# One encoder layer on one core: a new table for the order and the buffers of a kernel that replays its operations

## The chip, the cores and the metric

The kernel runs on one core of one Trainium2 chip. A core has TensorE (PE; its weight loads are listed as PEld), VectorE (DVE), ScalarE (ACT), GpSimd (POOL) and SyncE (SP), each with its own instruction queue, and 16 DMA engines, which SyncE, ScalarE and GpSimd issue transfers to. The metric is the device time of one execution in microseconds (us), as a median of several runs.

## The reference

One layer of a bidirectional encoder trunk in float32, for 512 rows of width 1024 (x is 1 x 512 x 1024):

```python
h = rmsnorm(x, mix_norm)
rx, ry, qkv, z, ba, gates = jnp.split(h @ w_in, SPLIT_IDX, axis=-1)
y_rnn = rglru_branch(rx, ry, ...) @ w_rnn_proj
y_dn = deltanet_branch(qkv, z, ba, ...) @ w_dn_proj
g_rnn, g_dn = jnp.split(jax.nn.sigmoid(gates), 2, axis=-1)
x = x + (g_rnn * y_rnn + g_dn * y_dn) @ w_out
h = rmsnorm(x, ffn_norm)
gt, up = jnp.split(h @ w_gate_up, 2, axis=-1)
x = x + (jax.nn.silu(gt) * up) @ w_down
return rmsnorm(x, final_norm)
```

The first branch is a short convolution, two sigmoid gates from block-diagonal matmuls and a linear scan in both directions. The second is a gated delta rule over 8 heads in chunks of 64 rows, in both directions; for each chunk it solves a unit triangular system of 64 x 64:

```python
A = jnp.where(strict, jnp.einsum("nhcid,nhcjd->nhcij", kb, k) * decay, 0.0)
lhs = A + jnp.eye(CHUNK)
u = triangular_solve(lhs, v * beta, lower=True, unit_diagonal=True)
w = triangular_solve(lhs, kb * exp(gc), lower=True, unit_diagonal=True)
```

## The kernel before

**What it computes on.** All matmuls with large operands work on pairs of a high and a low part (a value rounded to TensorE's faster float32 form, and the rest), so that three products stand for one in float32; several matrices are multiplied with seven block products in place of eight. Most matmuls are 128 x 128 weights on 128 x 512 or 128 x 256 columns. Buffers in SBUF are of two sizes, t2 (2 KB in each partition) and t4 (4 KB); a tile in PSUM is called ps and is one of eight banks. `hh` and `hl` hold the high and low part of the normalised, transposed input.

**The head.** SyncE and ScalarE load x in halves (`xl_`). While the first loads are on the way, TensorE does 16 matmuls of a matrix of ones on itself into a tile `idle`, whose result nobody reads. `load_gain` brings the norm's weights in as eight rows and transposes them (`gain1r`, `gain`). `raw_transpose` (L634) transposes x before it is normalised, four times 128 x 128 into one ps tile, and ScalarE copies the result, scaled by `gain`, into the high part `rhi` (float32 in the fast form), VectorE the rest into `rlo`; the first products (with the blocks of `w_in`) start from these. `rms_rstd` (L602) takes the squares (one half of the row on ScalarE, one on VectorE) and the root. The cast of a weight block into its high part is ScalarE's, too.

**The inverses.** `dn_inverse(g)` (L1052) inverts the triangular blocks of a group g of two heads; there are four groups. VectorE inverts the 32 x 32 diagonal blocks, TensorE puts them together: first 32 matmuls of 32 x 32 into a bank `pr`, a scaled copy of it by ScalarE, then 48 of 32 x 32 into two banks `px` and `pz`:

```python
for p8 in range(8):
    for b0 in (0, 2):
        for d, (i0, i1) in enumerate(((b0, b1), (b1, b0))):
            rr = R[32 * i1:32 * i1 + 32, 32 * p8:32 * p8 + 32]
            T.matmul(px[...], rr, yd(d, i1, p8), ..., tile_position=(32 * i1, 32 * i0))
            if b0 == 2 * d:
                T.matmul(pz[...], yd(d, i1, p8), rr, ..., tile_position=(32 * i1, 32 * i1))
```

then, after copies by ScalarE, 16 matmuls of 64 x 64 into `pr2` and 16 into `px2`. Each of these matmuls is in plain float32 and shows as two records in the trace; they take some hundredths of a microsecond each, where a matmul of 128 x 512 takes over two tenths. The same time of the program holds other work that TensorE does between them: products of `w_in` with `hh` and `hl`, transposes (`turn`, weights `ident`), products of the gates.

**Low parts by transfers.** The low parts of sums of weight blocks are made in place by transfers that GpSimd issues and that add to what the tile holds (rows `t<-t` POOLq in the profile).

**What sets the order.** No call to an engine runs at once. `Rec` records every call as an operation, in the order of the program's text, and `Plan.emit` (L482) issues them in the order of a table, `ORDER`, of 9257 numbers (each operation once). All engines' operations stand in this one list, so the list gives every engine's queue its order. A second table, `HOMES`, has for every t2, t4 and ps tile, in the order in which `new` (L546) draws them, the number of the buffer that it is put in; `emit` adds a wait where a tile takes a buffer whose last user was another engine. Both tables were found by a search outside the kernel. All instructions carry L516, the line of the recorder that runs the call.

Of the kernel before, what the change touches and what calls it, by code (L numbers as in the profile page):

```python
# [31 lines left out]
2061 0 2 3 5 2062 140 10 11 14 2063 2079 12 13 2080 1 2065 65 2099 2117 2100 7 234 2118 97 96 143 2064 2066 70 158 152  # L32
151 17 18 19 20 21 22 23 24 25 26 27 28 29 30 31 32 33 41 34 35 15 36 42 43 44 16 37 39 2067 2068 2073 2074 2075 2076
2069 2070 38 57 58 49 50 51 52 59 60 2077 2071 66 2081 45 2083 40 2072 2085 2078 2091 67 47 2082 2084 68 2092 2086
2087 2101 2102 71 72 69 73 75 74 312 53 77 2093 76 78 48 46 54 2103 61 55 62 56 2119 79 2094 2095 2088 2096 2111 2089
88 80 81 2098 2121 2090 2104 63 82 2097 9 85 89 84 92 64 93 83 2120 2122 90 86 2112 2113 2105 2106 2107 2108 2109 2110
2114 2115 2116 2123 2124 2129 2130 2131 2132 2125 2133 2134 390 363 2126 2127 159 160 235 2128 161 162 163 164 237 364
91 1123 1092 2138 418 3804 609 915 2142 94 313 87 2135 99 100 95 104 105 165 238 239 240 241 166 242 167 168 243 244
245 169 170 171 315 316 317 246 318 319 247 248 249 236 172 173 174 175 250 251 252 320 321 322 323 253 324 325 326
327 254 255 256 257 258 98 101 102 106 103 107 155 259 124 108 109 110 111 132 116 391 1124 314 125 328 133 117 134  # L40
126 135 127 118 119 392 2139 329 176 112 330 144 114 6 147 331 332 333 177 113 1093 142 141 146 157 145 122 123 115
260 334 335 336 337 261 365 136 120 121 128 130 138 156 131 137 129 139 3806 1126 262 1127 1128 178 179 338 339 180
181 340 1095 341 417 342 343 344 345 1096 263 264 265 266 267 268 1097 1098 3805 1099 269 270 271 272 273 274 182 183
346 347 184 348 148 349 350 275 149 276 277 278 351 352 185 186 187 188 1100 189 279 280 190 191 285 474 759 762 2136
760 150 1125 3807 203 286 192 1101 353 354 582 528 355 356 357 358 359 360 361 362 393 394 395 763 396 397 398 193
1102 1103 1104 1105 399 400 401 402 403 404 861 916 2140 367 2137 1247 2141 1031 1185 1000 368 1094 369 370 3808 768
583 216 281 282 283 194 195 196 197 284 289 205 610 371 1129 1130 1131 1132 198 199 200 204 206 287 207 584 405 290
201 475 1133 1134 1135 1136 1137 1138 1139 1140 1141 381 1142 1143 406 407 408 409 410 411 412 413 414 415 1144 372
888 862 291 366 288 208 292 864 416 865 529 421 3809 422 423 1106 373 385 386 387 382 1145 1146 1147 383 866 293 384
867 1107 1108 1109 1110 531 532 868 210 424 211 294 209 212 773 533 534 535 536 1111 388 295 374 869 307 308 309 213  # L50
214 215 218 870 375 376 537 807 3810 296 217 863 783 219 476 297 298 310 1112 299 300 301 1186 1113 1114 1115 419 425
636 377 378 889 667 420 379 530 764 1116 1117 871 872 873 1118 1119 1120 303 1148 1149 304 585 874 875 876 305 586 587
302 444 380 611 1150 877 769 306 445 588 589 538 765 439 590 591 592 426 431 432 433 593 594 595 612 440 389 434 448
435 436 774 770 539 766 767 771 772 441 437 1121 540 541 761 784 427 428 878 879 880 881 1151 1152 778 882 429 776 438
442 555 556 883 884 885 886 542 543 637 449 779 153 453 596 544 477 478 887 479 480 481 482 483 484 485 775 786 443
890 892 430 452 447 451 787 893 597 598 311 1187 894 154 895 780 1122 1216 545 599 600 601 788 1188 602 603 604 605
606 607 608 613 546 547 548 486 487 549 488 1189 1190 550 1191 551 1153 552 553 614 891 454 1192 1193 1194 1195 668
450 1196 554 1197 489 446 792 669 777 781 782 790 557 1001 797 490 1198 1199 1200 1201 1202 1203 1204 1205 670 671 672
673 674 675 676 677 678 679 680 681 682 683 684 685 686 1206 491 1207 1208 1209 492 493 789 791 615 502 3811 501 793
455 559 896 897 902 898 899 903 560 1248 468 798 1002 561 904 5595 562 616 558 799 563 564 8 617 905 494 495 496 497  # L60
498 499 500 505 910 911 912 1210 1211 913 577 578 1212 469 579 580 565 566 567 568 573 574 575 576 1249 506 1154 639
640 569 570 571 900 687 688 623 507 618 901 624 689 619 690 733 202 1066 906 572 691 692 693 907 625 626 620 908 909
621 785 794 802 581 470 917 472 803 1589 943 795 622 641 642 627 643 503 644 628 629 1250 1251 918 919 920 921 922 923
1252 456 508 462 942 944 509 924 694 914 631 632 1253 1254 1255 925 926 927 928 929 930 931 1256 1257 633 932 933 934
1258 1259 1260 1261 1262 1263 1264 1265 1266 1267 1268 511 935 936 937 1269 1270 1271 1272 734 808 810 811 812 645 646
647 796 698 800 801 805 804 806 1535 1534 457 458 504 463 464 471 466 473 510 1213 465 630 634 699 1032 938 939 940
834 835 700 1273 523 515 648 649 516 524 813 814 525 650 512 513 1214 517 1217 1274 1275 514 941 809 815 816 817 459
818 819 519 520 521 651 652 526 518 946 522 1588 1034 1003 820 821 822 823 824 825 826 827 828 829 830 701 1004 1005
831 1006 1035 653 654 1036 1037 1038 1039 1040 1041 945 638 1215 467 460 738 740 747 736 729 730 1007 655 656 657 658
659 660 661 1008 1009 1010 1011 1219 1012 732 735 737 3013 3014 739 1013 1014 1015 1016 1017 832 702 833 1220 1221  # L70
1222 703 838 1223 1224 1018 1019 1020 1021 1022 1023 1024 1025 1033 1225 1226 1042 1227 1043 969 1228 527 947 635 948
949 1218 748 461 836 1276 839 1026 970 731 749 950 840 841 951 1044 1045 1561 1643 1507 1046 1047 1048 1049 1050 1051
1052 750 1027 1508 842 1229 1230 1231 972 973 974 975 662 952 953 1232 1053 1054 1055 1056 1057 1233 1234 960 837 954
961 843 1277 971 1463 1397 704 705 751 964 706 707 965 708 709 966 752 1615 976 977 978 979 741 753 754 1235 742 755
757 756 663 955 1155 967 1562 1067 1236 1237 1238 1239 844 962 845 846 963 847 956 957 980 981 982 983 984 985 958 959
1058 710 711 1028 1156 1157 1240 1241 1242 1243 1158 1159 1160 1161 848 849 850 1162 856 857 852 858 859 853 854 1616
855 851 1063 986 987 988 989 990 991 992 993 994 995 1564 1565 1566 1510 1163 1164 1165 1166 1167 1567 1642 743 745
695 1509 1168 1169 1170 1171 1172 1173 1174 1175 1176 1177 1178 1179 1180 744 1062 746 1353 1354 1568 3015 1074 860
3016 664 1617 1563 665 1244 758 1059 1355 666 1590 1181 1511 1644 1029 1080 4 1070 1064 696 1065 1068 1512 1513 1514
1515 1516 1618 1619 1517 1245 968 1441 2148 1331 1620 1518 1519 1281 1520 1521 1569 1246 1522 1570 1571 1572 1573 1574  # L80
3017 3018 1575 3019 1576 712 713 714 715 716 717 718 719 720 721 722 1621 1622 1623 1624 1625 1626 1627 1628 1629 723
724 227 228 1577 1578 1332 2144 229 1579 1580 1030 1182 1398 725 1356 697 1523 1524 1581 1582 1357 1583 1584 1585 1586
1587 1075 1076 1078 1358 1525 1526 1527 1528 1529 1530 1531 1532 1533 3020 3021 3022 3023 3024 1334 1359 1630 1631
1183 996 997 726 230 2355 1669 2348 1069 1592 727 1184 1077 1593 728 1399 1594 1632 1633 1634 1635 1360 1536 1071 1464
1060 1072 1645 1595 998 3199 3025 1335 1636 1637 231 232 220 221 222 223 224 1638 1639 1640 1641 1336 1337 1338 1400
1401 1402 3026 3027 1403 1339 1361 1591 1081 1079 999 3198 1538 1646 1086 1061 3028 3029 1465 1333 3030 3031 3032 3033
3034 3035 3036 1647 1648 1362 1404 1405 1278 1280 1596 1539 1540 1279 1406 1407 1363 1364 1365 1597 1366 1367 1368
1340 1341 1342 1343 1344 1345 1346 1347 1348 1408 1409 1410 1411 1412 1369 1370 1349 1350 1351 1413 3037 3038 3039
# [1836 lines left out]
```

## Time and profile before

| what | us |
|---|---|
| median of 3 runs | 1040.49 |
| lowest and highest run | 1038.98, 1211.41 |
| the profiled execution | 1040.44 |
| its span, first to last instruction | 1038.7 |
| granted TensorE clock, mean | 0.997 |
| ScalarE busy | 730.5 (70%) |
| VectorE busy | 906.1 (87%) |

The profiled execution agrees with the median, so its rows can be used for the sum as they are. A row of the page names engine, tile written and read, shape, count, busy time and idle time ahead; a row of the chain has its start, its length and what it was; a row of the timeline gives start, length, engine, operation and count, and in brackets the idle time ahead of it and what ended it ("issue" when the trace shows nothing that it waited for). A row of a table by windows gives the stretch and its length, busy time and instruction count of the engines in it, the clock granted (1.00 is full), the DMA engines' share and GB/s.

### The profile page before, as it was taken

The page shows a single profiled execution, that of the slowest core. Times are in us where ns is not written, and L with a number is a line of the kernel's source. Part 1 is how long each engine was busy: PE and PEld are TensorE (multiplying, and loading weights), DVE is VectorE, ACT ScalarE, POOL GpSimd, SP SyncE. Part 2 cuts the span into 40 slices and gives each one's busy share as a digit, 9 for nine tenths or more (in the row PEclk, how much of TensorE's full clock was granted, in tenths as well). Part 3 has the DMA queues.
Part 4 walks back from the last instruction along what each step waited for, and adds up shares of the span by engine and source line. Part 5 has one row for each costly group of instructions (what it writes and reads, how often), then busy time and mean ns, then how long its engine had stood idle before and what let it go on. Part 6 is the DMA issues. An engine that isn't in the chain of part 4 may idle for free.

```text
span 1038.7 us, 18051 instructions
## 1 busy us (share of the span) xinstructions
PE 1028.2 (99%) x6675; PEld 902.0 (87%) x6675; DVE 906.1 (87%) x1699; ACT 730.5 (70%) x1331; POOL 91.1 (9%) x145
## 2 busy tenths in 40 slices
PE   9999999999999999999999999999999999999997
PEld 8988888888888888798888888889999999998886
DVE  6899998959896589659859979999999998999998
ACT  8699999998457766798897565578444544455674
POOL 6000000112000111142212000000000000000000
PEclk9999999999999999999999999999999999999999
DMA  9952442325644125979985636976555332256532
GB/s 300 308 159 85 144 120 85 90 56 127 183 96 122 50 80 151 267 177 219 232 222 134 183 114 213 304 217 200 166 174 173 118 102 82 83 203 198 180 109 81
DMA packets 185512, 163.75 MB, mean 158 GB/s; under 512 B 7728, under 2 KB 156352, under 8 KB 185424
## 3 DMA queue, kind: packets, MB, share of 16 engines
q1 hardware_dynamic: 178752, 144.37, 46.0%
q0 software_dynamic: 5344, 14.82, 7.9%
q10 hardware_dynamic: 1328, 3.42, 0.9%
q8 instruction: 52, 0.85, 0.3%
q14 instruction: 36, 0.29, 0.1%
HBM read 133.18 MB, written 18.91 MB: 146 GB/s over the span
## 4 chain that ended last, share of the span: by engine, by line
PE 98%; ACT 1%; DMA 0%; issue 0%; DVE 0%; ACTq 0%; DVEq 0%
PE ps L516 98%; ACT t L516 1%; DMA t<-in_w_in_dram 0%; ACTq L516 0%; DVE t L516 0%; ACT L516 0%; DVE na L516 0%; DVEq L1920 0%; DVE so L516 0%; ACT so L516 0%; ACT rst L516 0%; ACT warm L516 0%; DVE rin L516 0%
## 5 line engine op out<-in xcount | busy, mean ns | idle before, releaser
L516 PE MATMUL ps<-t,t 128*128 128x512 f32 (+3 forms) x3039 | 536.0, 322 | 2.5 <-issue 1.6
L516 DVE TENSOR_TENSOR t<-t,t 128x512 fp32r<-128x512 f32 (+19 forms) x807 | 506.3, 658 | 27.8 <-ACT t L516 13.4
L516 PEld LDWEIGHTS ps<-t,t 128*128 128x128 f32 (+1 forms) x3039 | 430.6, 180 | 58.2 <-issue 2.7
L516 PE MATMUL ps<-hh,t 128*128 128x512 f32 (+2 forms) x1680 | 456.5, 347 | 0.0
L516 ACT CAST t<-t 128x512 fp32r<-128x512 f32 (+2 forms) x400 | 298.0, 780 | 158.9 <-DVE t L516 60.5
L516 PEld LDWEIGHTS ps<-hh,t 128*128 128x128 f32 (+1 forms) x1680 | 298.1, 189 | 38.2 <-ACT t L516 0.2
L516 PE MATMUL ps<-hl,t 128*128 128x512 f32 (+2 forms) x848 | 278.6, 347 | 0.0
L516 PEld LDWEIGHTS ps<-hl,t 128*128 128x128 f32 (+1 forms) x848 | 158.4, 189 | 19.5 <-issue 0.2
L516 ACT ACT_TABLE_LOAD x73 | 93.7, 1283 | 12.0 <-DVE so L516 5.1
L516 DVE SCALAR_TENSOR_TENSOR t<-ps,par,t 128x511 f32<-128x511 f32 (+1 forms) x108 | 79.3, 744 | 14.7 <-ACT t L516 13.7
L516 ACT COPY t<-ps 128x512 f32<-128x512 f32 (+3 forms) x108 | 44.3, 429 | 52.7 <-PE ps L516 51.4
L516 ACT ACTIVATE t<-t 128x128 f32<-128x128 f32 (+5 forms) x114 | 72.6, 647 | 9.8 <-DVE t L516 8.0
L516 DVE TENSOR_TENSOR t<-ps,t 128x256 f32<-128x256 f32 (+1 forms) x106 | 50.3, 486 | 11.4 <-PE ps L516 8.7
L516 DVE TENSOR_TENSOR t<-t 128x512 f32<-128x512 f32 (+1 forms) x81 | 51.0, 636 | 0.9 <-DMA t<-in_w_out_dram 0.6
L516 ACT ACTIVATE t<-ps,par 128x512 f32<-128x512 f32 x68 | 45.8, 707 | 7.4 <-PE ps L516 7.2
L516 POOL TENSOR_SCALAR_AFFINE_SELECT t<-t 128x512 f32<-128x512 f32 x32 | 25.6, 807 | 218.5 <-DMA t<-gcr 107.5
L516 PE MATMUL ps<-t,na 128*128 128x128 f32 (+2 forms) x640 | 42.9, 232 | 0.0
L516 PEld LDWEIGHTS ps<-t,na 128*128 128x128 f32 (+2 forms) x640 | 39.6, 145 | 3.8 <-issue 1.4
L516 ACT ACTIVATE t<-ps 128x512 f32<-128x512 f32 (+1 forms) x58 | 28.7, 508 | 15.5 <-PE ps L516 15.0
L516 PE MATMUL ps<-ident,t 128*128 128x128 f32 (+1 forms) x200 | 32.4, 276 | 0.3 <-DVE t L516 0.3
L516 POOL DMA_DIRECT2D t<-t x20 | 18.1, 938 | 146.4 <-ACT t L516 131.3
L516 DVE SCALAR_TENSOR_TENSOR t<-ps,negc,t 128x128 f32<-128x128 f32 x48 | 13.7, 344 | 19.0 <-PE ps L516 18.9
(151 smaller groups left out, 612.4 us busy)
## 6 DMA issues: line engine op xcount, KB each, us to landing
t<-in_w_in_dram SPq DMA_DIRECT2D x70, 512.0 KB, 5.2
t<-in_w_gate_up_dram SPq DMA_DIRECT2D x44, 512.0 KB, 5.0
t<-in_w_down_dram SPq DMA_DIRECT2D x22, 512.0 KB, 4.9
t<-t POOLq DMA_DIRECT2D x20, 512.0 KB, 6.0
t<-in_w_down_dram SPq DMA_DIRECT2D x33, 256.0 KB, 3.8
t<-in_w_out_dram SPq DMA_DIRECT2D x12, 512.0 KB, 6.0
t<-in_w_rnn_proj_dram SPq DMA_DIRECT2D x16, 384.0 KB, 3.6
sums<-t SPq DMA_DIRECT2D x11, 512.0 KB, 4.1
```

Source lines behind the costliest of these rows:

```text
L516: self.plan.ops.append((self.eng, {x.tensor.name for x in aps}, outs, lambda: real(*a, **kw)))
```

## The change

The two tables have other numbers. The rest of the program is the same, text and operations. Of ORDER's and HOMES' rows, the first ones show how it looks:

```diff
 ORDER = """
-2061 0 2 3 5 2062 140 10 11 14 2063 2079 12 13 2080 1 2065 65 2099 2117 2100 7 234 2118 97 96 143 2064 2066 70 158 152
+2 0 17 18 19 20 21 22 23 5 3 2061 2062 10 11 14 1 2079 2080 13 12 2099 7 153 2100 2118 2117 234 96 2063 2064 70 2065
...
 HOMES = """
-1 3 2 4 3 0 10 17 11 18 1 2 7 6 5 7 6 8 9 0 10 12 13 11 14 7 6 8 0 2 1 30 2 0 7 6 0 0 9 23 1 12 6 2 14 1 14 1 4 7 6 1
+0 3 1 2 1 0 9 15 10 18 2 3 6 7 5 7 4 6 8 1 9 11 12 13 14 5 22 30 26 15 31 27 4 7 6 0 1 0 8 23 2 11 2 14 1 11 5 6 14 2
...
```

What it does is seen in the queues. The instructions of each engine are the same ones, but for four loads of ScalarE's tables fewer (69 for 73), which the order of functions decides.

**The head.** TensorE's queue before begins so (`ps_95` is the tile `idle`; `ps_102` and `ps_103` take the transposes of x, `t_88` and `t_90`; `ps_597` and `ps_598` are the first products, of weights `t_600` and `t_601` with the high part `t_98`):

```order
L516 MATMUL ps_95<-ones_83 128x128 x16
L516 MATMUL ps_102<-ident_78,t_88 128x128
L516 MATMUL ps_103<-ident_78,t_88 128x128
L516 MATMUL ps_102<-ident_78,t_90 128x128
L516 MATMUL ps_102<-ident_78,t_88 128x128
L516 MATMUL ps_93<-ident_78,gain1r_92 128x8
L516 MATMUL ps_102<-ident_78,t_90 128x128
L516 MATMUL ps_103<-ident_78,t_90 128x128
L516 MATMUL ps_103<-ident_78,t_88 128x128
L516 MATMUL ps_103<-ident_78,t_90 128x128
L516 MATMUL ps_597<-t_600,t_98 128x512
```

and after so:

```order
L516 MATMUL ps_95<-ones_83 128x128 x11
L516 MATMUL ps_93<-ident_78,gain1r_92 128x8
L516 MATMUL ps_95<-ones_83 128x128 x2
L516 MATMUL ps_102<-ident_78,t_88 128x128
L516 MATMUL ps_102<-ident_78,t_90 128x128
L516 MATMUL ps_102<-ident_78,t_88 128x128
L516 MATMUL ps_102<-ident_78,t_90 128x128
L516 MATMUL ps_95<-ones_83 128x128 x2
L516 MATMUL ps_103<-ident_78,t_88 128x128
L516 MATMUL ps_95<-ones_83 128x128
L516 MATMUL ps_103<-ident_78,t_90 128x128
L516 MATMUL ps_103<-ident_78,t_88 128x128
```

Five of the sixteen matmuls on ones now stand among the transposes, the gain's transpose comes first, and `ps_102` is complete before `ps_103` begins; one more transpose, and then the first products, follow. ScalarE's queue at the same place, before:

```order
L516 ACT_TABLE_LOAD
L516 CAST t_600<-t_599 128x512
L516 ACT_TABLE_LOAD
L516 ACTIVATE warm_87<-eps_t_86 128x1
L516 CAST t_600<-t_599 128x512
L516 ACTIVATE t_110,ssq_106<-t_88 128x512
L516 ACTIVATE t_116,ssq_112<-t_90 128x512
L516 ACTIVATE t_98<-ps_102,gain_94 128x256 x2
```

and after (the first cast is of half a weight block, the `ssq` rows are the squares, the last row the scaled copies):

```order
L516 ACT_TABLE_LOAD
L516 ACTIVATE warm_87<-eps_t_86 128x1
L516 CAST t_600<-t_599 128x512
L516 ACTIVATE t_116,ssq_112<-t_90 128x512
L516 CAST t_600<-t_599 128x512
L516 ACTIVATE t_110,ssq_106<-t_88 128x512
L516 ACTIVATE t_98<-ps_102,gain_94 128x256 x2
```

One table load is gone there (the next now comes some thirty rows later), and the two casts stand ahead of one square each. On SyncE's queue the second half of the second weight block (`t_602`) moves ahead of the second halves of x, which stood ahead of it.

**Group 1 of the inverses.** TensorE's queue before, with what each instruction waits for, at the start of the matmuls into `pr` (here `ps_805`; `t_802` and `t_803` are VectorE's inverses, `t_1003` is a low part added by a transfer of GpSimd):

```order
L516 MATMUL ps_1004<-hh_96,t_1003 128x512 [waits DMASW4_49]
L516 MATMUL ps_1004<-hh_96,t_1003 128x512
L516 MATMUL ps_1106<-hh_96,t_1104 128x512
L516 MATMUL ps_1004<-hh_96,t_1003 128x512 x4
L516 MATMUL ps_1106<-hl_97,t_1104 128x512
L516 MATMUL ps_1004<-hh_96,t_1003 128x512
L516 MATMUL ps_1106<-hh_96,t_1104 128x512
L516 MATMUL ps_1004<-hh_96,t_1003 128x512
L516 MATMUL ps_616<-t_619,t_621 128x512 [waits DMAHW6_49,PE_49]
L516 MATMUL ps_805<-t_802,na_789 32x32 [waits DVE_49,Activation_49]
L516 MATMUL ps_805<-t_803,na_789 32x32
```

and after:

```order
L516 MATMUL ps_1004<-hh_96,t_1002 128x512
L516 MATMUL ps_1004<-hl_97,t_1002 128x512
L516 MATMUL ps_1004<-hh_96,t_1003 128x512 [waits DMASW6_49]
L516 MATMUL ps_1004<-hh_96,t_1003 128x512 x7
L516 MATMUL ps_805<-t_802,na_789 32x32 [waits DVE_49]
L516 MATMUL ps_805<-t_803,na_789 32x32
```

The product with the DMA's block `t_619` has gone elsewhere, and of the waits ahead of the run two are left. Further on, the 48 matmuls into `px` and `pz` (`ps_808`, `ps_807`) ended before with

```order
L516 MATMUL ps_808<-t_806,t_803 32x32
L516 MATMUL ps_808<-t_806,t_802 32x32
L516 MATMUL ps_883<-ident_78,t_867 128x128
L516 MATMUL ps_1106<-hl_97,t_1104 128x512
L516 MATMUL ps_1106<-hh_96,t_1104 128x512
L516 MATMUL ps_616<-t_620,t_621 128x512
L516 MATMUL ps_617<-t_619,t_621 128x512
L516 MATMUL ps_616<-t_619,t_622 128x512 x2
L516 MATMUL ps_617<-t_620,t_621 128x512
L516 MATMUL ps_617<-t_619,t_621 128x512
L516 MATMUL ps_809<-t_804,na_789 64x64 x16
```

and are now split, 31 of them ahead of this piece and 17 behind its long matmuls:

```order
L516 MATMUL ps_808<-t_806,t_803 32x32
L516 MATMUL ps_808<-t_806,t_802 32x32
L516 MATMUL ps_883<-ident_78,t_867 128x128
L516 MATMUL ps_1106<-hl_97,t_1104 128x512
L516 MATMUL ps_616<-t_620,t_621 128x512
L516 MATMUL ps_1106<-hh_96,t_1104 128x512
L516 MATMUL ps_1106<-hl_97,t_1104 128x512
L516 MATMUL ps_616<-t_619,t_621 128x512
L516 MATMUL ps_616<-t_620,t_621 128x512
L516 MATMUL ps_1106<-hh_96,t_1104 128x512
L516 MATMUL ps_616<-t_619,t_622 128x512 x2
L516 MATMUL ps_617<-t_619,t_621 128x512
```

**Group 0.** Before, the run into `pr` (`ps_692`) was followed by a transpose and then by 50 long matmuls before the run into `px` (`ps_695`) and `pz`, of which these are the first:

```order
L516 MATMUL ps_692<-t_689,na_676 32x32
L516 MATMUL ps_692<-t_690,na_676 32x32
L516 MATMUL ps_770<-ident_78,t_754 128x128
L516 MATMUL ps_589<-t_560,t_591 128x512
L516 MATMUL ps_589<-t_524,t_592 128x512
L516 MATMUL ps_589<-t_530,t_592 128x512
```

Now eight are left between the two runs:

```order
L516 MATMUL ps_692<-t_690,na_676 32x32
L516 MATMUL ps_771<-ident_78,t_754 128x128
L516 MATMUL ps_569<-t_548,t_572 128x512
L516 MATMUL ps_569<-t_554,t_572 128x512
L516 MATMUL ps_866<-hl_97,t_864 128x512
L516 MATMUL ps_866<-hh_96,t_864 128x512
L516 MATMUL ps_866<-hl_97,t_864 128x512
L516 MATMUL ps_569<-t_560,t_572 128x512
L516 MATMUL ps_866<-hh_96,t_864 128x512
L516 MATMUL ps_866<-hl_97,t_864 128x512
L516 MATMUL ps_695<-t_693,t_690 32x32
L516 MATMUL ps_695<-t_693,t_689 32x32
```

In groups 0, 1 and 3 single transposes now also stand inside the short runs; in group 2 the 64 x 64 matmuls into `pr2` follow the run into `px` and `pz` at once, where before twelve long matmuls stood between, and six long ones are left between `pr2` and `px2`, where eight were.

858 rows, old and new, of tables (HOMES, ORDER) are left out of this document.

## The prediction, made before the run

> **What bounds the kernel now.** I read the page first, for shares, then the chain that ended last, then the waits of TensorE, and last the timeline and the windows around each place where the chain leaves TensorE. The page:
>
> ```profile
> span 1038.7 us, 18051 instructions
> PE 1028.2 (99%) x6675; PEld 902.0 (87%) x6675; DVE 906.1 (87%) x1699; ACT 730.5 (70%) x1331; POOL 91.1 (9%) x145
> ```
>
> TensorE is busy 99% of the span. The chain, in order of time (start, length, what):
>
> ```profile
> 0.80 3.91 DMA t<-in_w_in_dram
> 4.74 0.62 ACT t L516
> 5.37 1.28 ACT L516
> ...
> 9.03 417.90 PE ps L516 x2289
> 426.93 1.60 issue
> 428.53 197.78 PE ps L516 x1534
> ...
> 633.00 398.49 PE ps L516 x2665
> ```
>
> So the whole execution is one queue of matmuls, with three places to win: the 9.03 us ahead of the first long matmul, a hole of 1.60 us at 426.93, and 1038.7 - 1031.5 = 7.2 us of tail. The other engines only matter where they hold TensorE up, and that is little: the first row below is the hole, the second lies ahead of 9.03.
>
> ```profile
> PE ps L516 <- issue: 1.6, 1, 1.6
> PE ps L516 <- ACT t L516: 0.9, 1, 0.9
> ```
>
> **The change part by part.** Only the order of the 9257 operations and their buffers change; TensorE has the same matmuls. How long they take does not depend on the order where they stand back to back:
>
> ```profile
> 50.00:100.00 50.00, 50.00 (x222) 1.00 0.44 139
> ```
>
> 222 long matmuls in 50 us are 0.225 us each, with the clock at 1.00 and other engines and DMA at work beside them. The thousands of places at which matmuls change their neighbours I cost at nothing: what hides them is this queue itself, as long as operands are there; without that cover each shows as a new wait. What the order saves on VectorE or ScalarE elsewhere (four loads of ScalarE's tables fewer, among others) lies beside this queue and is 0 too. So is the tail: its last matmuls and the chain behind them stand in the same order.
>
> The head first. Before:
>
> ```profile
> 1.08 5.84 PE L516 MATMUL ps<-ones 128*128 128x128 f32 x32 [1.08 <-POOL ones L516]
> 6.75 0.60 PE L516 MATMUL ps<-ident,t 128*128 128x128 f32 x4
> 9.03 1.19 PE L516 MATMUL ps<-t,t 128*128 128x512 f32 x4 [0.93 <-ACT t L516]
> 4.74 0.62 ACT L516 CAST t<-t 128x512 fp32r<-128x512 f32 x1 [1.60 <-DMA t<-in_w_in_dram]
> 7.29 0.62 ACT L516 ACTIVATE t<-t 128x512 f32<-128x512 f32 x1
> 7.91 0.61 ACT L516 ACTIVATE t<-t 128x512 f32<-128x512 f32 x1
> 8.52 0.81 ACT L516 ACTIVATE t<-ps,gain 128x256 fp32r<-128x256 f32 x2
> ```
>
> TensorE waits for ScalarE's scaled copies at 8.52, and these stand behind two squares and, in the chain above, a table load of 1.28. In the new order ScalarE has no second table load ahead of the squares, but cast (4.74), square, cast, square, scaled copies. At some 0.6 from start to start the copies come at 4.74 + 4 x 0.6 = 7.1, and the first is done at about 7.5. TensorE's own list is then the longer one. Its matmuls there:
>
> ```profile
> 5.00:7.00 2.00, 2.00 (x19) 1.00 0.98 348
> ```
>
> 19 records in 2 us are 0.11 each; a warm-up matmul is two records. The sixteen warm-ups ended at 6.75, so eleven end at 6.75 - 10 x 0.11 = 5.65. Then come the gain's small transpose (7.29 to 7.44 before: 0.15), two warm-ups (0.44), four transposes (0.45), two warm-ups (0.44), and four transposes with one warm-up among them (0.66): 5.65 + 2.14 = 7.8, and the first long matmul at 7.9, a gain of 1.1. The transposes need the last of the first two halves of x to be there by 6.24. All that the rows tell is that it was there by 6.75, where it was transposed; then it is 8.4 and the gain 0.6. The other end is ScalarE's 7.5, a gain of 1.5. I take 1.1: that half of x is the third load on SyncE's queue as before, and nothing is put ahead of it. **Head: -1.1.** What comes later in the head (more x halves behind more weights on SyncE's queue) is covered by the long matmuls of the first weights.
>
> The hole at 426.93 lies inside the block inverse of group 1 (start, length, what; each of these short matmuls leaves two records):
>
> ```profile
> 424.41 0.75 PE L516 MATMUL ps<-t,na 32*32 32x32 f32 x64
> 425.10 0.33 PE L516 MATMUL ps<-ident,t 128*128 128x128 f32 x1
> 425.18 0.70 PE L516 MATMUL ps<-t,t 128*128 128x512 f32 x2
> 425.72 0.49 PE L516 MATMUL ps<-ident,t 128*128 128x128 f32 x3
> 426.14 0.79 PE L516 MATMUL ps<-t,t 32*32 32x32 f32 x62
> 428.53 0.67 PE L516 MATMUL ps<-t,t 32*32 32x32 f32 x34 [1.60 <-issue]
> ...
> 432.53 1.15 PE L516 MATMUL ps<-t,na 64*64 64x64 f32 x32
> ```
>
> No engine is waited for: the run of 96 stops after 62. The page counts 52 transfers on the instruction queue:
>
> ```profile
> q8 instruction: 52, 0.85, 0.3%
> q8 instruction: 1, 0.02, 2.5%
> ```
>
> The first row is the whole span, the second the window from 426.1 to 428.53 alone; the window from 411 to 426.1 has none. TensorE has 2 x 6675 = 13350 instructions (weight load and matmul), so a transfer holds about 13350/52 = 257, or 128 records. 128 records back from the stop is 424.46, four records into the first short run. So that block of instructions was eaten in 426.93 - 424.46 = 2.5 us, while the next was in only at 428.53, 4.1 us after the block's start. Blocks of long matmuls last 128 x 0.225 = 29 us, and hide this. [...]
>
> The hole costs more than itself:
>
> ```profile
> 428.60:432.00 3.40, 3.40 (x42) 2.76 (x43) 3.37 (x8) 2.65 (x8) 0.00 (x0) 0.50 1.12 251
> 341.65 1.26 PE L516 MATMUL ps<-t,t 32*32 32x32 f32 x96
> 342.84 0.77 PE L516 MATMUL ps<-ident,t 128*128 128x128 f32 x5
> ```
>
> For 3.40 us behind it the granted clock is 0.50: half of 3.4, 1.7 us, is lost. From the start of the run (426.14) to 432.53 are 6.39 us; the same run in group 0 took 342.84 - 341.65 = 1.19, a transpose 0.1, eight long matmuls 1.8: 3.1. So hole and clock cost 3.3 together. [...] The row shows the slow clock behind 1.60 us. The hole of 0.93 us at 9.03 had none, so the border lies between.
>
> In the new order the run of group 1 is broken after 62 records, right at the block's end, so the block itself is as short as before: 2.5 us. What moves is what stands ahead of it. Before, the last long matmul waits for a DMA and for TensorE itself, and the first short one, right behind, for VectorE and ScalarE. Now the first short one waits for VectorE alone, and the next wait ahead is eight long matmuls back. VectorE's last transpose ahead of the run was:
>
> ```profile
> 421.52 0.71 DVE L516 STREAM_TRANSPOSE t<-t 128x512 f32<-128x512 f32 x1
> ```
>
> It ended at 422.23. If a block is asked for once the sequencer, which runs ahead of TensorE, has passed the start of the one before, those waits held the request until 422.2 or later, and the data were there 6.3 us after it. With the sequencer free there, the request goes out up to a full lead earlier. The hole ends if it goes out 1.6 us sooner (4.1 - 2.5). Bounds: 0 (it stays) and 3.3 (it goes, with the slow clock). Of these I take 3.3, because the row it is nearest to is that of all the other blocks, which show no hole. What is late next, if VectorE should be, is the same short run. **Group 1: -3.3.**
>
> Now the other inverses. They change too. Counted in the order from the stop above (every 128 records), the block in group 0 now holds the end of one short run, eight long matmuls, and 82 records of the next run: 115 x 0.0124 + 8 x 0.225 + 5 transposes x 0.14 = 3.9 us; before, it held 42 long matmuls and lasted some 10.6 us. Group 2's holds 77 records of 32x32, 42 of 64x64, 6 long matmuls and 3 transposes: 0.95 + 42 x 1.08/32 + 1.35 + 0.4 = 4.1 us; group 3's, by the same sum, 3.3. What a fetch needs there:
>
> ```profile
> 332.03 0.40 PE L516 MATMUL ps<-hh,t 128*128 128x512 f32 x1
> q8 instruction: 1, 0.02, 2.3%
> 517.00:524.17 7.17, 7.17 (x124) 1.00 0.87 264
> q8 instruction: 1, 0.02, 2.4%
> ```
>
> In group 0 (first two rows) the block began at 332.03 and its transfer came in the window 334.5 to 337: 2.5 us later, and with the 2.4 us that the one at 426.1 took, 4.9. In group 2 (the other two) the block began at about 516.8, its transfer came in the window 519.5 to 522: 2.7 + 2.4 = 5.1. Against 3.9 and 4.1 that leaves waits of 1.0 in each. A request that goes out earlier, as in the blocks of long matmuls, leaves 0; the 4.1 us of group 1 leave 0.2 and 0; a fall of the clock adds 1.7 to one that passes 0.93. I take 1.0 for group 0, 0.5 for group 2 and 0.3 for group 3. **New waits: +1.8.**
>
> **The sum.** 1040.44 (the profiled execution; its span is 1038.7, the rest lies around it; the median of the runs, 1040.49, is the same) - 1.1 - 3.3 + 1.8 = 1037.8.
>
> **The rivals.**
>
> The hole stays in group 1: the block is as short as before, and if the request is sent only as the block starts, or the hole is no fetch, breaking the run changes nothing there. For it: the stop fell at the very instruction where the next block begins, and that does not move; VectorE's wait is still there. Against it: three of the four waits ahead are gone. 1040.44 - 1.1 = 1039.3 without new waits, 1041.1 with all of the 1.8.
>
> The hole moves to group 0 in full: if its fetch needs more than 4.9 us, the wait passes 0.93 and brings the slow clock: 1.6 + 1.7 = 3.3 in place of 1.0, so 1037.8 + 2.3 = 1040.1. For it: 332.03 against 334.5 with a half-empty DMA. Against it: no wait of TensorE stands at the start of that block any more.
>
> Slower, because POOL's adding transfers land late: the low parts of some weights come by transfers that POOL issues and that add in place:
>
> ```profile
> t<-t POOLq DMA_DIRECT2D x20, 512.0 KB, 6.0
> t<-t POOLq DMA_DIRECT2D x2, 512.0 KB, 10.3
> ```
>
> Over the span they take 6.0 us in the median; the two between 411 and 426.1 took 10.3. The new table moves their readers. A reader placed 6 us behind such an issue in that stretch waits 4.3 us, and 1.7 more for the clock: 1037.8 + 6.0 = 1043.8. Against it: TensorE's waits name none of them before. From 2.6 us of such waiting, clock included, the change is slower than before.
>
> **How the numbers follow.** Forecast (hole gone, short new waits): 0.5, from 1036.0 (no new wait) to 1039.2. Hole stays: 0.24, 1039.3 to 1041.1. Hole moves in full: 0.12, 1039.7 to 1041. Late adding transfers: 0.08, 1040.5 to 1044. No new wait and a head of -1.5 or a little more: 0.06, under 1035.6. The range 1035.0 to 1041.2 leaves out most of the fourth and some of the last. About 2% (20.8 us) is what a measurement of this kernel can tell from no change; no case comes near it, so within 2% has 0.97, faster 0.02 (a saving that no row shows), slower 0.01 (late transfers at all twenty places).
>
> **What would show it.** Head: first long matmul at about 7.9 and no wait for ScalarE of 0.9. Group 1: no "issue" piece between 420 and 430 and a clock of 1.00 there. New blocks: "issue" waits of up to 1 us inside the short runs of groups 0 and 2, with an instruction transfer in them. It is wrong if the hole is still there, if a wait for POOL's queue or a DMA shows on TensorE, or if the long matmuls no longer keep 0.225 us.

## The result, and the profile after

The changed kernel takes 1046.06 us (median of 4 runs, 1045.27 to 1047.17), the kernel before 1039.80; the ratio is 1.0064, 95% interval [1.0044, 1.0083]. It is slower by 6 us, within 2%, and outside the range that was predicted (1035.0 to 1041.2, 1037.8 likeliest). The ratios here and below leave out one slow run each of the kernel before (1211.41 us) and of a_shift80 (1489.16 us). The profiled execution took 1047.17, its span 1045.5. It is the longest of the four, with the lowest mean clock (0.995, the others 0.996 to 0.997), so what the profile shows of a low clock is at the upper end.

The page of the kernel after, first lines:

```profile
span 1045.5 us, 18043 instructions
PE 1033.5 (99%) x6675; PEld 905.8 (87%) x6675; DVE 909.3 (87%) x1699; ACT 726.7 (70%) x1327; POOL 99.4 (10%) x145
```

TensorE is still full, with as many instructions as before, and busy 5.3 us longer: a busy TensorE at half its clock counts as busy (3.40 of 3.40 us from 345.8 on, at 0.50, below). What TensorE waited for, in all, times, longest:

```profile
PE ps L516 <- issue: 2.8, 2, 2.2
PE ps L516 <- DMA t<-t: 1.2, 1, 1.2
PE ps L516 <- POOL eps_t L516: 1.1, 1, 1.1
PE ps L516 <- DVE t L516: 0.3, 1, 0.3
```

The wait of 0.9 for ScalarE in the head is gone; the "issue" waits were one of 1.6 and are two, together 2.8; one for a transfer is new. The larger hole lies in group 0 (timeline of the kernel after; start, length, what):

```profile
341.91 0.82 PE L516 MATMUL ps<-t,t 32*32 32x32 f32 x58
342.66 0.55 PE L516 MATMUL ps<-ident,t 128*128 128x128 f32 x3
343.14 0.39 PE L516 MATMUL ps<-t,t 32*32 32x32 f32 x24
345.72 0.42 PE L516 MATMUL ps<-t,t 32*32 32x32 f32 x12 [2.19 <-issue]
```

It stands behind 58 + 24 = 82 records of the run, where the prediction had counted the block's end. From 345.1 on, where the hole still lasts, the clock is low for 6.8 us; behind the hole of the kernel before it was 3.4 (windows; stretch and length, busy, clock):

```profile
345.80:349.20 3.40, 3.40 (x50) 0.50 0.56 166
349.20:352.60 3.40, 3.40 (x11) 0.60 0.00 0
345.10:351.90 6.80, 6.18 (x57) 0.50 0.39 121
```

The third row takes it whole: half the clock for 6.8 us, of which TensorE worked 6.2. Matmuls of 128 x 512 start 0.43 us apart there (349.95 to 351.66) and 0.23 behind it (357.01, 357.24), so I estimate the loss at half of 6.2, some 3.1 us.

The smaller one is what is left of the hole in group 1:

```profile
431.61 0.84 PE L516 MATMUL ps<-t,t 32*32 32x32 f32 x61
433.06 0.21 PE L516 MATMUL ps<-t,t 32*32 32x32 f32 x1 [0.61 <-issue]
```

And the head (same view; first long matmul at 8.69, 9.03 before):

```profile
6.25 1.14 PE L516 MATMUL ps<-ones 128*128 128x128 f32 x4
7.22 0.60 PE L516 MATMUL ps<-ident,t 128*128 128x128 f32 x4
...
8.69 2.77 PE L516 MATMUL ps<-t,t 128*128 128x512 f32 x11
```

Both kernels leave 6675 records of matmuls on TensorE, so the n-th record of one can be set against the n-th of the other. With the undisturbed time of the records ahead of each taken off (the two orders differ), the kernel after lags by:

| up to record | time before, after (us) | lag of after (us) | step |
|---|---|---|---|
| 1536 | 326.5, 326.6 | 0.12 | the head gives nothing in the end |
| 1920 | 361.2, 367.0 | 5.64 | group 0: +5.5 |
| 2304 | 424.9, 430.0 | 5.66 | |
| 2432 | 432.7, 436.5 | 3.67 | group 1: -2.0 |
| 2688 | 463.7, 469.4 | 6.00 | around the wait for the transfer: +2.3 |
| 4096 | 652.6, 659.3 | 6.77 | groups 2 and 3 and their neighbourhood: +0.8 |
| 6656 | 1027.7, 1034.4 | 6.79 | nothing |

The sum is the difference of the two profiled executions, 1047.17 - 1040.44 = 6.7.

### The profile page after: what moved, and what is told of

Read it like the earlier page. It is cut to its first block, busy times and chain, and to the rows that moved or that the text cites. A ratio compares the mean times of both kernels' runs of the same rounds, so it can differ in the third digit from the quotient of the medians.

```text
span 1045.5 us, 18043 instructions
## 1 busy us (share of the span) xinstructions
PE 1033.5 (99%) x6675; PEld 905.8 (87%) x6675; DVE 909.3 (87%) x1699; ACT 726.7 (70%) x1327; POOL 99.4 (10%) x145
## 4 chain that ended last, share of the span: by engine, by line
PE 54%; DVE 5%; DMA 2%; issue 1%; ACT 0%; DVEq 0%; POOLq 0%
PE ps L516 54%; DVE t L516 5%; DMA t<-t 1%; DMA zs<-t 1%; DMA osums<-t 1%; DVE na L516 1%; ACT t L516 0%; DVEq L1920 0%; ACT rst L516 0%; DVE nq L516 0%; DVE rin L516 0%; DVEq L516 0%; POOLq L516 0%
## 5 line engine op out<-in xcount | busy, mean ns | idle before, releaser
L516 PE MATMUL ps<-hh,t 128*128 128x512 f32 (+1 forms) x1680 | 455.1, 348 | 0.0
L516 PEld LDWEIGHTS ps<-hh,t 128*128 128x128 f32 x1680 | 297.7, 189 | 38.6 <-ACT t L516 0.3
L516 ACT ACT_TABLE_LOAD x69 | 88.5, 1283 | 12.8 <-DVE t L516 9.1
L516 POOL TENSOR_SCALAR_AFFINE_SELECT t<-t 128x512 f32<-128x512 f32 x32 | 29.7, 941 | 323.3 <-DVE t L516 207.0
L516 PE MATMUL ps<-t,na 128*128 128x128 f32 (+2 forms) x640 | 45.0, 237 | 0.4 <-DVE t L516 0.3
L516 POOL TENSOR_SCALAR t<-t,dnse 128x128 f32<-128x128 f32 x48 | 26.1, 610 | 44.3 <-ACT t L516 29.2
```

The source lines that it names most:

```text
L516: self.plan.ops.append((self.eng, {x.tensor.name for x in aps}, outs, lambda: real(*a, **kw)))
```

## The experiments

| kernel | edit | median | before, same chip | ratio, 95% |
|---|---|---|---|---|
| b_shift48 | before, 48 TensorE instructions more | 1039.05 | 1040.35 | 0.9992 [0.9984, 1.0001] |
| b_shift256 | before, 256 more | 1044.25 | 1040.35 | 1.0039 [1.0025, 1.0053] |
| b_break | before, group 1's run broken | 1042.05 | 1040.35 | 1.0017 [1.0008, 1.0026] |
| a_shift80 | after, 80 more | 1042.33 | 1040.35 | 1.0019 [1.0010, 1.0028] |
| a_late | after, transfers near group 0 later | 1043.26 | 1040.52 | 1.0035 [1.0023, 1.0047] |
| b_g0 | before, short block in group 0 | 1039.95 | 1040.52 | 0.9998 [0.9989, 1.0007] |
| a_shift80_read | a_shift80, readers later | 1042.26 | 1040.52 | 1.0021 [1.0011, 1.0031] |
| b_free | before, 48 more in the head's wait | 1038.82 | 1040.52 | 0.9989 [0.9980, 0.9998] |
| b_late | before, transfers near group 1 later | 1041.74 | 1039.58 | 1.0016 [1.0007, 1.0024] |
| a_late_read | a_late, readers later | 1042.73 | 1039.58 | 1.0032 [1.0021, 1.0043] |
| b_head | before, one operation of the head moved | 1039.98 | 1040.48 | 0.9998 [0.9989, 1.0006] |
| b_head_free | b_head and b_free | 1038.71 | 1040.48 | 0.9987 [0.9978, 0.9996] |

### Is the hole a late block of instructions?

If it is, it hangs on where the boundaries of the 256-instruction blocks fall, and more instructions ahead of it move them. b_shift48 adds twelve small matmuls, 48 instructions:

```diff
+    for _ in range(12):
+        T.matmul(idle[0:32, 0:32], ones[0:32, 0:32], ones[0:32, 0:32], start=True, stop=True, tile_position=(0, 0))
     with tc.manual_schedule():
         plan.emit()
# ORDER
-... 30 31 32 33 41 34 ...
+... 30 31 32 9257 9258 9259 9260 9261 9262 9263 9264 9265 9266 9267 9268 33 41 34 ...
```

> The kernel before, with twelve 32 x 32 matmuls of ones on ones behind the sixteen warm-ups, into the same unread tile: 48 more TensorE instructions (each such matmul is two loads and two matmuls), so that every boundary of the 256-instruction blocks falls 48 instructions earlier in the program. Theory 1, the hole at 426.93 is a block of instructions that comes too late because the block before it is eaten in 2.5 us: the shortest block of the whole program is now 4.6 us, the hole of 1.6 us and the half clock behind it (3.3 us together) are gone or under 0.5 us; the new matmuls cost 24 x 0.012 to 0.024 = 0.3 to 0.6 us at the most, and lie ahead of ScalarE's work in the head, which sets the end there. Time 3.3 - 0.3 = 3 us under before, 1036.8. Theory 2, the hole belongs to these matmuls (an operand, a bank, a semaphore): it stays at the same matmul, 62 records into the run, and the time is that of before, 1039.8 to 1040.1.

b_shift256 is the same with 64 (operations 9257 to 9320):

> The same with 64 small matmuls, 256 instructions: every boundary falls where it was, one whole block later. Control for the one with twelve. Theory 1: the hole is still there at the same matmul, 1 to 2 us, with the half clock behind it; time as before plus what the 128 records cost (128 x 0.012 = 1.5 us at most, less what ScalarE's work in the head covers, 0.9): 1040 to 1041. Theory 2: the same. A hole that is gone here too would speak against both.

and a_shift80 adds 20 to the kernel after, behind operation 27:

> The changed kernel, with twenty 32 x 32 matmuls behind its first eleven warm-ups: 80 more instructions, boundaries 80 earlier. Shortest blocks now 4.5 us (group 3), 5.4 (group 0), 5.7 (group 2); they were 2.4 (group 1), 3.2 (group 3), 3.8 (group 0). Theory 1: the hole of 2.2 us in group 0 and the low clock behind it (5.3 us together by the comparison of the traces), and the 0.6 us in group 1, go; the small matmuls cost 40 x 0.012 to 0.024 = 0.5 to 1.0 us in the head. Time 1046.1 - 5.9 + 0.7 = 1041, with the wait for the adding transfer at 450 (1.2 us) still there. Theory 2: the holes stay at their matmuls, 1046.1 + 0.7.

Group 1 with 48 instructions more (b_shift48), the run whole:

```profile
426.16 0.49 PE L516 MATMUL ps<-ident,t 128*128 128x128 f32 x3
426.58 1.16 PE L516 MATMUL ps<-t,t 32*32 32x32 f32 x96
427.67 0.33 PE L516 MATMUL ps<-ident,t 128*128 128x128 f32 x1
```

With 256 more (b_shift256), the hole again, behind 62 records:

```profile
431.49 0.79 PE L519 MATMUL ps<-t,t 32*32 32x32 f32 x62
433.85 0.47 PE L519 MATMUL ps<-t,t 32*32 32x32 f32 x34 [1.58 <-issue]
```

Group 0 of the kernel after, with 80 more (a_shift80):

```profile
343.37 0.55 PE L517 MATMUL ps<-ident,t 128*128 128x128 f32 x3
343.85 0.52 PE L517 MATMUL ps<-t,t 32*32 32x32 f32 x36
344.30 0.55 PE L517 MATMUL ps<-ident,t 128*128 128x128 f32 x3
```

The 24 and 12 records that the hole parted are one run of 36. Theory 1 stands: the hole goes with a shift, and comes back with a shift by a whole block. The times were mis-sized. A record of a small matmul among the warm-ups took 0.031 us, not 0.012 to 0.024, so a matmul cost 0.06: 64 of them put the first long matmul from 9.03 to 12.94. A low clock is not the reason, since the warm-ups just ahead of them were already 0.11 us apart. Why they take longer than those in the run into px (0.012) was not shown; unlike those, all of them stand at one `tile_position`. In b_shift256 the low clock also stood elsewhere, not behind the hole but in the head, behind 6.8 us in which TensorE was busy throughout with the small matmuls and the transposes:

```profile
5.90:12.70 6.80, 6.80 (x149) 1.00 1.05 360
12.80:16.10 3.30, 3.16 (x8) 0.50 1.07 372
433.90:437.30 3.40, 3.40 (x75) 1.00 1.12 251
```

In a_shift80 the fall from 1046.06 is 3.7 us, with 0.7 paid in the head (8.69 to 9.37). In b_shift48, with 0.5 paid, the profiles show TensorE 2.7 us ahead behind group 1 and only 1.7 ahead from about 536 on: until 530.91 it waits for ScalarE,

```profile
530.91 1.16 PE L516 MATMUL ps<-t,t 128*128 128x128 f32 x8 [0.28 <-ACT t L516]
```

which had waited 1.22 us for a load of w_in, until 525.87, and had not come forward with TensorE. A microsecond of the gain was given back there.

### Does breaking the run do it?

b_break takes only group 1's break from the change:

```diff
# ORDER: 3709 5056 5057 2153 2156 2154 2155 2157 2158 (a transpose, eight long matmuls) stand behind 3264
-... 3261 3263 3264 3265 ... 3280 3284 3709 ... 5056 5057 2153 ... 2157 2158 3299 ...
+... 3261 3263 3264 3709 5056 5057 2153 2156 2154 2155 2157 2158 3265 ... 3280 3284 ... 3299 ...
```

> The kernel before, with nothing changed but group 1's run of 48 short matmuls, broken after 31 as in the changed kernel: the transpose and the eight long matmuls that stood behind it now stand ahead of its last 17. Theory 1 (late instruction block): the block that is eaten ahead of the hole is the same 2.5 us, so the hole is still there after 62 records, with the same cost; 1039.8, within 0.5. Theory 3 (the run itself is too long, and breaking it lets the fetch catch up): hole gone, 3.3 us less, 1036.5.

The hole was still there ("issue", one of 1.6 us, at the same record), and a new wait of 1.1 us for ScalarE, which now had the last 17 results later than before: 1.7 us slower. So theory 3 falls. What made group 1's hole smaller in the changed kernel was not the break.

### Is the block too short, or its fetch late?

a_late leaves TensorE's order and takes transfers out of the way of the fetch in group 0:

```diff
# ORDER of the kernel after: 1973 3080 2207 2149 (SyncE) stand behind 3623, 2163 (GpSimd) behind 3369
-... 2475 1973 3080 2163 3557 ... 2207 2511 ... 2019 2149 3623 2562 ... 3369 3585 ...
+... 2475 3557 ... 2511 ... 2019 3623 1973 3080 2207 2149 2562 ... 3369 2163 3585 ...
```

> The changed kernel; only six transfers that were issued from 336.9 to 339.3, just ahead of and around the request for group 0's block of instructions, stand later in the order (one block of the projection of the first branch, one broadcast row, two sums of weight blocks, and GpSimd's adding transfer of a block of w_in), behind the load that was issued at 341.55. TensorE's order is untouched, so the block in group 0 is eaten in the same 3.8 us. Theory A (the block is too short for any fetch): the hole in group 0 stays, 1 to 2.2 us, time within 1 us of the changed kernel, 1046. Theory B (the fetch came late because its packets stand behind those transfers): its packets start about 1 us after the request in place of 4.5, the hole is gone or under 0.5 us, the low clock with it, and the time falls by up to 5.3 us, to 1041.

(The edit moves five transfers, not six.) The DMA queues of the kernel after, from 334 to 343.2 and from 343.2 to 345.8 (packets of all, then the instruction queue; packets, MB, share of 16 engines):

```profile
DMA packets 1303, 1.37 MB, mean 149 GB/s; under 512 B 32, under 2 KB 837, under 8 KB 1303
...
DMA packets 866, 0.81 MB, mean 313 GB/s; under 512 B 53, under 2 KB 617, under 8 KB 865
q8 instruction: 1, 0.02, 2.3%
```

and of a_late from 339.1 to 341.7:

```profile
DMA packets 1, 0.02 MB, mean 6 GB/s; under 512 B 0, under 2 KB 0, under 8 KB 0
q8 instruction: 1, 0.02, 2.2%
```

A block of instructions is a single packet. With nothing else under way it was through in 0.022 x 16 x 2.6 = 0.92 us, and it started 1.0 us after TensorE was 48 instructions ahead of the start of the block before the one fetched. No packet of this kind starts ahead of that point in any of the traces (the earliest 0.6 us behind it; counted with 40 in place of 48, five packets of the kernel before and two of the kernel after do, by up to 0.24 us), so I take it for the first moment at which a block can be asked for. In stretches of long matmuls packets start up to 4.8 us ahead of that block in the kernels before and after. In the kernel after the packet started at 343.24, 4.5 us after that moment. The run is whole and the clock full in the profile of a_late:

```profile
342.60 0.52 PE L516 MATMUL ps<-t,t 32*32 32x32 f32 x36
...
342.80:346.20 3.40, 3.40 (x80) 1.00 1.07 298
```

Yet the median fell by 2.8 us, not by the 5.3 of theory B. In the profile, which took 1042.60, a new wait of 0.88 us for ScalarE stands at 370.44, and the wait for the adding transfer is 1.71 us (1.24 in the kernel after). And three of the eight runs took 1044.7 to 1046.8 us with a mean clock of 0.995 or 0.996, where the other five had 0.999. They have no trace; whether the hole came back in them was not shown.

b_g0 is the other half of the pair: the short block, put into the kernel before, where DMA is idle:

```diff
# ORDER of the kernel before: 2479 to 2510 (the matmuls into pr) and 2511 (the copy) stand behind 1949
-... 2052 2479 2480 ... 2509 2510 2981 2053 ... 2059 2207 2511 3077 ... 1948 1949 2020 ...
+... 2052 2981 2053 ... 2059 2207 3077 ... 1948 1949 2479 2480 ... 2509 2510 2511 2020 ...
```

> The kernel before; only the 32 short matmuls into pr of group 0 and ScalarE's copy of their result stand later, so that ten long matmuls are left between them and the run into px (50 before, eight in the changed kernel). The block of instructions there is eaten in 3.7 us (10.3 before). DMA was nearly idle there in the profile of before (0.31 of the 16 engines from 329.3 to 342.6). Theory A: a hole of 1 us or more opens in group 0 beside the one in group 1; 1040.4 + 1 to 5. Theory B: with idle DMA the block is there in time, no hole in group 0; 1040.4 within 0.7.

```profile
339.84 0.73 PE L516 MATMUL ps<-t,t 128*128 128x512 f32 x2 [0.48 <-ACT t L516]
340.41 0.40 PE L516 MATMUL ps<-hl,t 128*128 128x512 f32 x1
340.65 1.79 PE L516 MATMUL ps<-hh,t 128*128 128x512 f32 x7
342.36 1.26 PE L516 MATMUL ps<-t,t 32*32 32x32 f32 x96
```

No hole, though the block was eaten in 4.4 us, with the wait in the first row (4.6 in the kernel after, up to its hole); the hole in group 1 was there as ever. The fetch started 1.1 us after its first moment. Theory B holds for group 0: the block is short and its fetch is late, and it takes both.

b_late tries the same in group 1 of the kernel before, where the block lasts 2.5 us:

```diff
# ORDER of the kernel before: 5050 2222 (GpSimd) stand behind 3372, 2225 (SyncE) behind 3802
-... 2183 5050 3795 ... 2164 2222 5056 ... 3372 2225 3802 3689 ...
+... 2183 3795 ... 2164 5056 ... 3372 5050 2222 3802 2225 3689 ...
```

> The kernel before; only two of GpSimd's transfers (an adding one issued at 417.6, a block of w_in issued at 423.8) and one load of SyncE's (issued at 424.0) stand later, behind group 1's run into px. TensorE's order is untouched: the block of instructions in group 1 is still eaten in 2.5 us, at the same place. Theory B (the fetch is late because it queues behind transfers): with part of them gone the packets start earlier than 3.8 us after the request, the hole at 427 is gone or under 0.5 us and the low clock with it: 1040.5 - 2.4 = 1038.1, up to 1 us of it given back behind 530 as in the runs with twelve small matmuls. Theory A (2.5 us are too short for any fetch): the hole stays, 1040.5.

It tells nothing on the theories: GpSimd, which runs ahead, issued the two only 1.5 us later (419.14 for 417.64, 425.28 for 423.80), the fetch started no earlier (427.55 for 426.12), the hole stayed (1.8), and in the profile a new wait of TensorE for ScalarE of 1.0 and a half clock of 6.8 us in place of 3.4 made it slower. Whether idle DMA alone would close group 1's hole was not shown.

### The wait for the adding transfer

In the kernel after TensorE waits 1.24 us, until 451.74, for a transfer that GpSimd issued at 444.56 and that landed 7.14 us later (chain of waits, then timeline):

```profile
444.56 7.14 DMA t<-t
451.74 48.55 PE ps L516 x267
451.74 0.97 PE L516 MATMUL ps<-t,t 128*128 128x512 f32 x3 [1.24 <-DMA t<-t]
```

In two runs its first readers were put later:

```diff
# ORDER of the kernel after: 2195 2196 2197 2198 stand behind 5074
-... 3362 3360 2195 2196 2197 2198 3364 ... 5073 5074 3403 ...
+... 3362 3360 3364 ... 5073 5074 2195 2196 2197 2198 3403 ...
```

> The changed kernel with the twenty small matmuls, and four matmuls that read a block whose low part is made by an adding transfer moved seven long matmuls later. If the wait of 1.8 us at 445 is for that transfer and nothing else is late behind it, it goes and the time is 1042.3 - 1.9 = 1040.4. If the chain of the state updates, whose small matmuls now come 0.9 us earlier, has no slack, part of it comes back as a wait for VectorE: 1041 to 1042.

> The changed kernel with both edits: the six transfers around group 0 later, and the four matmuls that read the late low part seven long matmuls later. Group 0 has no hole, and the wait of 1.7 us at 445 is gone; by what the readers' edit showed alone, waits for ScalarE and VectorE of about 1 us come in its place. 1043.3 - 1.0 = 1042.3, still over the kernel before. If it comes to 1040 or less, the adding transfer was all that was left.

The wait went, and others took most of its place (a_late_read):

```profile
444.67 1.16 PE L516 MATMUL ps<-t,na 128*128 128x128 f32 x8 [0.19 <-DVE t L516]
...
448.11 1.38 PE L516 MATMUL ps<-t,t 128*128 128x128 f32 x10 [0.91 <-ACT t L516]
```

The times did not move beyond their intervals (1.0021 after 1.0019, 1.0032 after 1.0035). The transfer was not the only operand that comes too late there in the new order; the others come from ScalarE and VectorE.

### The head, and a version under both

b_head and b_head_free move one operation; b_free and b_head_free have the twelve small matmuls behind the head's transposes (behind operation 44), where TensorE waits anyway:

```diff
# ORDER of the kernel before
-... 11 14 2063 2079 ... 2080 1 2065 ...
+... 11 14 1 2063 2079 ... 2080 2065 ...
```

> The kernel before with the twelve small matmuls, now behind the transposes of the head, where TensorE waits 0.9 us for ScalarE. The boundaries are those of the run with twelve behind the warm-ups. If the first long matmul was late there only because the small ones delayed the transposes, it starts at 9.03 again, and the time is 1039.05 - 0.5 = 1038.5, under both kernels; no hole in group 1.

> The kernel before with one operation moved: ScalarE's first activation (the root of one constant, whose result nobody reads) stands ahead of its first cast, as in the changed kernel, so that the second load of a table (1.28 us) in the head falls away. TensorE's order is untouched. ScalarE's squares then start when the loads of x are there (6.3) in place of 7.3, the scaled copies at about 7.5 to 7.9, after TensorE's transposes (done at 8.1); first long matmul at 8.2 to 8.6 in place of 9.03, and later by up to 0.7 where TensorE's clock goes up late. If that gain holds to the end, time is 0.5 us under before; if the loads of the weights behind it set the pace, it is lost again within the first 50 us.

> The same, with the twelve small matmuls behind the transposes of the head, so that the boundaries of the instruction blocks fall as in the run that had them there (1038.8). TensorE's list in the head is now the longer one, and the small matmuls cost 0.3 to 0.6 us of what the table load gave. 1038.8 less 0 to 0.5: 1038.5, no hole in group 1, under both kernels.

With the second table load away the first long matmul came at 8.50 (b_head), 9.03 before; the time did not move beyond its interval. By the traces 0.50 of the 0.53 us was still there ahead of group 1; but the fetch there started when it did before (426.07 for 426.12), so the hole was 1.9 us in place of 1.6, and less than 0.1 was left behind it. With the small matmuls 9.25 and 8.63, and no hole. b_head_free, 1038.71, is 0.13% under the kernel before, with the interval under 1, and 0.7% under the changed one.

## Why the prediction was wrong

**The bound** was read rightly: TensorE's queue, and only its holes count.

**The head, -1.1:** mis-sized, and then lost. The first long matmul came at 8.69 (predicted 7.9). The rows of the clock are 1.00 throughout, but the records tell when TensorE gets fast: 0.21 us apart until 5.3 in the kernel before, until 7.2 in the kernel after (windows of one microsecond; records in each):

```profile
5.00:6.00 1.00, 1.00 (x6) 1.00 1.00 350
6.00:7.00 1.00, 1.00 (x5) 1.00 1.03 373
7.00:8.00 1.00, 1.00 (x11) 1.00 1.05 404
```

I had taken the fast records of one profile as the rule. With the same head, a_late began its long matmuls at 8.17 and a_late_read at 7.82, which would have met the forecast; their records get fast at 5.4 and 4.4. So whether 7.9 comes true hangs on a point that the order does not set: with one order in the head it lay at 4.4, 5.4 and 7.2 us in these three profiles. What sets it was not shown. Of the 0.34 us that the profile gained nothing was left at record 1536.

**Group 1, -3.3:** -2.0. That the hole is a late block of instructions was right (the shifts), and that the break itself would do nothing (b_break). That the request would go out up to a full lead earlier did not show: the fetch started 6.3 us after its first moment in both kernels (419.79 to 426.12, 424.51 to 430.77). Counted from the block's start it came at 1.2 us in place of 1.7, the block lasted 2.9 us in place of 2.5, and 0.61 us of hole remained. In a_late, with the same order of TensorE, the fetch started 5.2 us after its first moment, and there was no hole.

**New waits, +1.8:** the step that failed. Group 0 had 1.0 in the sum, and cost 5.5: a hole of 2.2, and 6.8 us of low clock in place of none. I took the fetch's start in the kernel before, 2.5 us after the block's start, and carried it over to a short block: 2.5 + 2.4 = 4.9 us against 3.9. After the change the fetch started 4.3 us after the block's start (338.95 to 343.24), the next block was in 6.8 us after it, and the block was eaten in 4.6.

The step was wrong because a fetch does not go by the block's start. Counted from the first moment, with TensorE 48 instructions ahead, it started 4.8 us later in the kernel before (329.75 to 334.55) and 4.5 us later in the kernel after (338.76 to 343.24), so this delay hardly changed. But those 48 instructions took 2.5 us before, where long matmuls are among them, and 0.2 us after, where all of them are short. In the kernel after the delay came from the traffic, which the change had moved there too: a_late, with the same order of TensorE, had 1.0 us and no hole. From 338.8 to 343.2 the DMA share is 0.95 in the kernel after, and neither the lead nor the traffic was set into the sum:

```profile
338.80:343.20 4.40, 4.40 (x141) 1.00 0.95 195
329.70:332.80 3.10, 3.10 (x56) 1.00 0.00 0
```

The second row is the kernel before: there the DMA engines were idle for the first 3.1 of the 4.8 us, so traffic alone does not explain that delay, and what held that fetch stays open. The rival "the hole moves to group 0 in full" had the mechanism, with 0.12 and 3.3 us; it put the loss by the low clock at 1.7 us, where some 3.1 were lost. And the border of the clock between 0.93 and 1.60 us, which it used, is no border of length: behind waits of 1.71 us (a_late) and 1.78 us (a_shift80) and a hole of 1.58 us (b_shift256) the clock was 1.00. Groups 2 and 3, with 0.5 and 0.3 in the sum, showed no hole (a_late_read has one of 0.43 us in group 2); that 0.8 us were lost in their neighbourhood all the same is a coincidence.

**The adding transfers:** the rival on the other side, with 0.08. One of them was late, by 1.24 us; its surroundings cost 2.3.

**Tail and steady rate:** as predicted, 0.00 from record 4096 to the end but for 0.02.

So two rivals came true beside each other, and the range was built as if only one would. What stays open: what of the 2.3 us around 445 would be left if each wait there were removed in turn, the 0.8 us of groups 2 and 3, and what holds a fetch back where the DMA engines are idle.

## What to carry to other kernels

Where TensorE is full, its own instruction stream can be the bound (a hole of 1.6 us in the kernel before, of 2.2 and 0.6 in the kernel after): a stretch in which 256 instructions take less than the 4.5 + 2.4 = 6.9 us that a fetch took under load in group 0 needs its next block asked for early, and that fetch is one packet among all the transfers that are under way. What counts is also what stands just ahead of the block: 48 short matmul instructions gave a lead of 0.2 us, 48 with long ones among them 2.5. Look for "issue" holes inside runs of short matmuls, count blocks from one hole to find the next, and check what the order has DMA do there; a few cheap instructions ahead, in a wait that exists anyway, move every boundary (48 in b_free: the first long matmul at 9.25 for 9.03, and no hole). And a reordered program must be read in all queues: in group 0 the short block alone (b_g0) and a late fetch behind a long block (the kernel before) left no hole, and both together cost 5.5 us.

## What the runs showed of the hardware

- A block of 256 instructions (TensorE's 13350 came in 52 packets) is one packet on the instruction queue, 0.92 us long when alone, and TensorE went on about 2.4 us after its start (426.1 to 428.53; 343.24 to 345.72). In group 0 it started 4.5 us after the first moment under load (the kernel after) and 1.0 and 1.1 with idle DMA (a_late, b_g0); in the kernel before it started 4.8 us after it, with idle DMA for the first 3.1. With blocks of short matmuls the fetch showed as holes of 1.6 and 2.2 us, which went with the block boundaries.
- A low clock does not follow from the length of a hole. The clock was 0.50 for 3.4 us or more behind holes of 1.56 to 2.19 us (b_break, the kernel before, b_late, b_g0, b_head, the kernel after), and 1.00 behind a hole of 1.58 us (b_shift256) and waits of 1.71 and 1.78 us (a_late, a_shift80). In b_shift256 it was 0.50 from 12.8 us on, behind a stretch in which TensorE was busy throughout, most of it with small matmuls.
- Of 31 runs of the kernel before on one chip 12 had a mean clock of 0.999, with a median of 1039.1, and 19 less, with 1040.8. The 1.7 us between them is what a half clock for 3.4 us costs by my estimate (half of it); these runs have no trace, so that the hole was there in all of them is a guess. The kernel before has two times, and a difference of one microsecond to it must be looked at with this in mind.
